# Sixteen quartered pairs of w_up in a row, on sums of its quarters that transfers build in DRAM

## The chip, the cores and the metric

The kernel runs on one core of a Trainium2 chip. The metric is the device time of one execution in microseconds (us). TensorE is PE below, VectorE DVE, ScalarE ACT, GpSimd POOL; SP issues most transfers, and a DMA issued by an engine stands in that engine's order of instructions.

## The reference

One trunk layer of a decoder: x is 512 tokens by 1024 columns, all float32. First attention (a sparse mixer and an RWKV mixer on one combined projection, gated together, an output projection, a residual add), then the channel sub-layer, in which the change lies:

```python
def conv_ffn(h, w_up, conv_w, conv_b, w_down):   # h: 512 x 1024, w_up: 1024 x 5632
    u = h @ w_up
    up = jnp.pad(u, ((0, 0), (CONV_WIDTH - 1, 0), (0, 0)))
    c = conv_b + conv_w[0] * up[:, 0:s]
    for j in range(1, CONV_WIDTH):
        c = c + conv_w[j] * up[:, j:j + s]
    val, gate = jnp.split(c, 2, axis=-1)
    return (jax.nn.silu(gate) * val) @ w_down
```

## The kernel before

Float32 products are made of two parts: a value is split into a rounded high part (an ACT copy) and a low part (value minus high part, a subtraction on DVE or POOL), and a product is three: high by high, high weight by low operand, low weight by high operand.

**The up projection** works on 22 pairs, n = 0 to 21. Pair n has one index f and takes a gate tile and a value tile of 128 columns of w_up (columns 2816 + 128 f and 128 f). A **dense pair** is two `dense_fm` calls of 24 matmuls, each 512 tokens wide. A **quartered pair** (`quartered`) sees the two tiles as a 2 by 2 matrix of quarters: B11 and B12 are the upper 512 rows of w_up for gate and value, B21 and B22 the lower 512. With sums of quarters on both sides seven products do the work of eight; each product is 12 matmuls of 256 tokens. The sums of the tokens' side are made once (`token_sums`, over the first pairs). The weights' side needs T1 = B11 + B12, T2 = T1 + B22, T2 - B11 (which is B12 + B22), and T2 + B21. Before, `wload` loads the upper quarters into two columns of the tile `right` (or a `raw` buffer) and the lower into a `raw` buffer; an adding transfer of POOL (L289) makes T1, and three DVE additions (in `first_quarters` and `quartered`) make the rest. Which pairs are quartered stands in the table `QUARTERED`: n = 5, 6, 8, 9, 11, 12, 14, 15, 17, 18 and 20, two quartered and one dense in turn. After each pair come a causal convolution over tokens (`conv`: one ACT and two DVE instructions for each tile), silu, a product into a column of `right`, and every second pair `sums` for the down projection.

**Buffers.** `right` has 11 columns; columns that hold finished values are copied to DRAM (`kept`, POOL, L1752), lent to the loads, and read back at the end. There are three `raw` buffers, taken in turn, for every weight of the kernel. SP's order of loads is fixed, and a load waits until its buffer is free; a load that waits holds up those behind it.

**Attention** comes first and takes its weights by the same `wload` and `raw` buffers. POOL has work of its own there: low parts of some weight tiles (`wlo<-raw,whi`), some fills (`inv`, whose second half Tn starts a triangular inverse that DVE then runs as a chain), small transfers between partitions (`KH`, `KL`, `Vr`, `sq`). Except in stretches written out by hand, a scheduler fixes each engine's order when the kernel is built.

Of the kernel before, what the change touches and what calls it, by code (L numbers as in the profile page):

```python
# [24 lines left out]
KT = D // 128  # L25
# [58 lines left out]
def hybrid_block(ctx: ExitStack, tc: tile.TileContext, A: dict, out: bass.AP):  # L84
# [133 lines left out]
    hl = hp.tile([128, KT, S], F32R, name="hl", tag="hl")  # L218

    order = [f for i in range(NFH) for f in (i, NFH + i)]  # L220
    QUARTERED = {5: None, 6: 6, 8: 0, 9: 6, 11: 0, 12: 2, 14: 0, 15: 2, 17: 0, 18: 2, 20: 0}

    def weight_tiles():
        def cols(w, o, kt=KT, eng=v):
            return w[:, o:o + 128], kt, 128, eng

        def rows(w, o, n, kt=KT, eng=v):
            step = 1024 // n
            for i, k0 in enumerate(range(0, kt, step)):
                kn = min(step, kt - k0)  # L230
                yield w[128 * k0:128 * (k0 + kn), o:o + n], kn, n, eng[i] if type(eng) is list else eng

        pool_ = nc.gpsimd
        yield cols(w_in, O_RWKV + 1536, eng=pool_)
        yield cols(w_in, O_RWKV + 1664, eng=pool_)
        for p in range(NH2):
            for o in (512, 0, 1024):
                yield cols(w_in, O_RWKV + o + 128 * p)
        yield cols(w_in, O_KC)
        yield from rows(w_in, O_Q, 512, eng=[v, pool_, ("spare", pool_), v])  # L240
        yield cols(w_in, O_VC)
        yield from rows(w_in, O_KS, 256, eng=[v, ("spare", v)])
        for m in range(NGA):
            yield cols(w_in, O_GA + 128 * m)
        yield from rows(w_in, O_KW, 280, eng=pool_)
        for m in range(NGA, KT):
            if m < 4:
                for s4 in range(m if m > NGA else 0, m + 1):
                    for s_ in "kv":
                        yield A["cmp_w1_" + s_][0][512 * s4:512 * s4 + 512], 4, 256, "ab" if (s4, s_) == (3, "k") else None  # L250
            yield cols(w_in, O_GA + 128 * m)
        for m in range(NGB):
            yield cols(w_in, O_GB + 128 * m)
        for m in range(KT):
            if m + NGB < KT:
                yield cols(w_in, O_GB + 128 * (m + NGB), eng=pool_ if m else v)
            yield cols(A["w_proj_b"][0], 128 * m, NH2, eng=pool_)
        for m in range(KT):
            yield cols(A["w_proj_a"][0], 128 * m, NH2)
        yield from rows(A["w_out"][0], 0, 512)  # L260
        yield from rows(A["w_out"][0], 512, 512, eng=())
        for n_, f in enumerate(order):
            if n_ in QUARTERED:
                for kh in range(2):
                    yield A["w_up"][0][512 * kh:512 * kh + 512], KT, 128, ("quarters", f, kh, QUARTERED[n_])
            else:
                yield cols(A["w_up"][0], DFF + 128 * f)
                yield cols(A["w_up"][0], 128 * f)

    wtiles = weight_tiles()  # L270
    loads, ahead, late, behind, spent, slots = [], [], [], [], [], itertools.count()
    def wload():
        nxt = next(wtiles, None)
        if nxt is None:
            if spent:
                spent[0]()
        else:
            src, kt, n, eng = nxt
            if eng == "ab":
                raw, eng = AB[:, 0].rearrange("p a r t -> p (a r t)").rearrange("p (k n) -> p k n", n=n), None  # L280
            elif type(eng) is tuple and eng[:1] == ("quarters",) and not eng[2] and eng[3] is not None:
                raw = right[:, eng[3]:eng[3] + 2].rearrange("p a (k n) -> p (a k) n", n=n)
            else:
                raw = wp.tile([128, kt, n], F32, name="raw", tag=f"raw{next(slots) % 3}", bufs=1)
            if type(eng) is tuple and eng[:1] == ("quarters",):
                for i, c0 in enumerate((DFF + 128 * eng[1], 128 * eng[1])):
                    nc.sync.dma_start(raw[:, 4 * i:4 * i + 4], src[:, c0:c0 + 128].rearrange("(k p) n -> p k n", p=128))
                if not eng[2]:
                    nc.gpsimd.dma_start(raw[:, 4:8], raw[:, 0:4], accum_op=ALU.add)  # L289
                eng = "quarters"  # L290
            else:
                nc.sync.dma_start(raw, src.rearrange("(k p) n -> p k n", p=128))
            loads.append((raw, kt, n, eng))

    def wsplit():
# [8 lines left out]
    def wsplit_():  # L304
        if loads:
# [2 lines left out]
                ahead.append(raw)  # L308
                return
            if eng == "quarters":  # L310
                wload()
                ahead.append(first_quarters(raw, loads.pop(0)[0]))
                return
            if type(eng) is tuple:
                eng = eng[1]
# [1177 lines left out]
    def token_sums():  # L1493
        for kh in range(2):
            def total(o, K, i):
                ks, ns = slice(4 * K + 2 * kh, 4 * K + 2 * kh + 2), slice(256 * i, 256 * i + 256)
                tt(o, hh[:, ks, ns].bitcast(F32), hl[:, ks, ns].bitcast(F32), ALU.add)

            x, y, z, w = [right[:, i].rearrange("p (k n) -> p k n", k=2) for i in range(3, 7)]
            total(x, 0, 1)  # L1500
            total(y, 1, 1)
            tt(y, y, x, ALU.subtract)
            yield
            total(z, 0, 0)
            tt(x, z, x, ALU.subtract)
            stt(z, y, -1.0, z, ALU.mult, ALU.subtract)
            yield
            total(w, 1, 0)
            stt(w, w, -1.0, z, ALU.mult, ALU.subtract)
            for j, o in enumerate((y, z, x, w)):  # L1510
                hi, lo = sum_parts(j, kh)
                act(hi, o)
                tt(lo, o, hi.bitcast(F32), ALU.subtract)
                if j % 2:
                    yield
# [18 lines left out]
    def by_quarter(w):  # L1534
        return w.rearrange("p (q k) n -> p q k n", q=2)

    def first_quarters(top, low):
        b11, t1, b22 = top[:, 0:4], top[:, 4:8], low[:, 4:8]
        hi, lo = two_quarters()
        halves(hi, lo, by_quarter(top))  # L1540
        t2 = pb().rearrange("p (k n) -> p k n", k=4)
        tt(t2, b22, t1, ALU.add)
        tt(b11, t2, b11, ALU.subtract)
        y = 2 * (next(turnsq) % 2)
        t3 = [split[y + j][:, :, NFH - 3].rearrange("p q (k n) -> p q k n", k=2) for j in range(2)]
        halves(*t3, by_quarter(b11))
        return t2, low, (hi, lo), t3

    def quartered():
        t2, low, (h0, l0), (h3, l3) = ahead.pop(0)  # L1550
        b21 = low[:, 0:4]
        G, V, W = mmb(), mmb(), pa()[:, 0:256]
        act(V[:, 0:256], kc[:, 0:256], AF.Copy, scale=0.0)
        U = hB[:, 256 * (NFH + 3):256 * (NFH + 5)]
# [10 lines left out]
            for k in range(4):  # L1565
                mm_on(o, los[k], moving(j, k)[0], False)

        wload()
        h1, l1 = two_quarters()
        with tc.high_priority():  # L1570
            halves(h1[:, 0], l1[:, 0], t2)
            halves(h1[:, 1], l1[:, 1], b21)
        product(W, h0[:, 0], l0[:, 0], -1, True)
        act(G[:, 0:256], W)
        product(V[:, 0:256], h0[:, 1], l0[:, 1], 0)
        act(V[:, 256:512], V[:, 0:256])
        h2, l2 = two_quarters()
        tt(b21, t2, b21, ALU.add)
        halves(h2, l2, by_quarter(low))
        product(W, h1[:, 0], l1[:, 0], 1)  # L1580
        act(U[:, 0:256], W)
# [286 lines left out]
```

## Time and profile before

| | us |
|---|---|
| three runs | 803.55, 803.65, 804.17 |
| median | 803.65 |
| the profiled execution's own time | 803.25 |
| its span, first to last instruction | 801.5 |
| PE busy in it | 794.1 (99%) |
| DVE busy | 641.5 (80%) |
| ACT busy | 468.3 (58%) |
| POOL busy | 79.3 (10%) |

The up projection's quartered stretch lies between 515 and 692 us of the span. Busy time is the time in which an engine had an instruction running; consecutive instructions overlap a little, so what one instruction costs its engine is read from the distance of two starts.

### The profile page before, as it was taken

To read this page: it belongs to the slowest core of one execution; us is meant where nothing else is said; L and a number is where in the kernel's file an instruction comes from. 1 tells how busy PE (TensorE), PEld (TensorE's weight loads), DVE (VectorE), ACT (ScalarE), POOL (GpSimd) and SP (SyncE) were. 2 spreads that over 40 slices of the span, in tenths; PEclk is the share of its full clock that TensorE was granted. 3 is DMA by queue.
4 is the path that set the end of the run, shared out by engine and by line. 5 is a ranking of instruction groups with operands and counts; after the bars stand their busy time and mean duration, and the time that the engine had idled before them with its cause. 6 is when DMAs were issued, how large, how long until landed. Compare 5 with 4: busy or idle time off the path is not lost.

```text
span 801.5 us, 14688 instructions
## 1 busy us (share of the span) xinstructions
PE 794.1 (99%) x5649; PEld 667.3 (83%) x5649; DVE 641.5 (80%) x1240; ACT 468.3 (58%) x958; POOL 79.3 (10%) x115
## 2 busy tenths in 40 slices
PE   8999999999999999999999999999999999999998
PEld 7777788987777887787788898899999999788886
DVE  6477869993665578889685489999999989998895
ACT  6766654563444567778344365576676666546452
POOL 6200011032000044011000000101010000000010
PEclk9999999999999999999999999999999999999999
DMA  8433313237562241000158323574354434676821
GB/s 241 115 79 79 79 53 105 72 81 199 152 108 78 58 91 54 15 27 27 55 181 292 102 69 106 147 194 116 111 153 127 128 82 144 200 245 211 285 96 53
DMA packets 117123, 96.42 MB, mean 120 GB/s; under 512 B 5317, under 2 KB 99452, under 8 KB 116540
## 3 DMA queue, kind: packets, MB, share of 16 engines
q1 hardware_dynamic: 111344, 84.93, 36.7%
q0 software_dynamic: 4656, 8.07, 4.4%
q10 hardware_dynamic: 1052, 2.48, 1.0%
q8 instruction: 44, 0.72, 0.4%
q14 instruction: 27, 0.22, 0.1%
HBM read 84.45 MB, written 6.49 MB: 113 GB/s over the span
## 4 chain that ended last, share of the span: by engine, by line
PE 93%; DVE 3%; ACT 1%; DMA 1%; issue 1%; POOL 0%; DVEq 0%; POOLq 0%; ACTq 0%
PE ps_mm L123 58%; PE ps_mm L126 11%; PE ps_a L126 8%; PE ps_a L123 7%; PE ps_b L123 4%; PE ps_b L126 2%; PE ps_b L1306 1%; DMA pra<-in_rwkv_ln_b_dram 1%; PE ps_mm L1306 1%; DVE P L1232 0%; POOL pra L170 0%; DVE P L136 0%; DVE wlo L132 0%; ACT P L129 0%; ACT whi L129 0%
## 5 line engine op out<-in xcount | busy, mean ns | idle before, releaser
L123 PE MATMUL ps_mm<-hh,whi 128*128 128x512 f32 (+1 forms) x448 | 174.1, 391 | 0.5 <-DVE hl L141 0.5
L129 ACT ACTIVATE whi<-raw 128x1024 fp32r<-128x1024 f32 (+3 forms) x119 | 112.3, 948 | 102.2 <-PE ps_mm L123 66.4
L123 PE MATMUL ps_mm<-hl,whi 128*128 128x512 f32 (+1 forms) x448 | 171.9, 386 | 0.0
L325 DVE TENSOR_TENSOR wlo<-raw,whi 128x1024 fp32r<-128x1024 f32 (+1 forms) x67 | 77.5, 1159 | 40.5 <-ACT whi L129 20.8
L123 PE MATMUL ps_mm<-hh,wlo 128*128 128x512 f32 (+1 forms) x448 | 108.6, 382 | 0.0
L123 PEld LDWEIGHTS ps_mm<-hh,whi 128*128 128x128 f32 x448 | 84.2, 188 | 20.1 <-issue 1.3
L123 PEld LDWEIGHTS ps_mm<-hl,whi 128*128 128x128 f32 x448 | 84.3, 188 | 16.0 <-issue 1.0
L123 PEld LDWEIGHTS ps_mm<-hh,wlo 128*128 128x128 f32 x448 | 82.1, 188 | 16.6
L141 DVE SCALAR_TENSOR_TENSOR right<-ps_mm,cw,right 128x511 f32<-128x511 f32 (+1 forms) x64 | 45.9, 744 | 0.1
L132 DVE TENSOR_TENSOR wlo<-raw,whi 128x1024 fp32r<-128x1024 f32 (+1 forms) x39 | 40.7, 1043 | 5.1 <-ACT whi L129 4.8
L129 ACT ACTIVATE P<-P,nm 128x512 f32<-128x512 f32 (+3 forms) x64 | 35.5, 556 | 11.3 <-DVE nm L1232 10.9
L325 POOL TENSOR_TENSOR wlo<-raw,whi 128x512 fp32r<-128x512 f32 (+3 forms) x13 | 20.9, 1607 | 176.7 <-PE ps_mm L123 142.5
L1232 DVE CUSTOM_DVE_ANT_0 P<-ps_a,AB 128x512 f32<-128x512 f32 (+3 forms) x64 | 29.4, 486 | 1.8 <-PE ps_a L123 1.5
L129 ACT ACTIVATE right<-ps_mm,cw 128x512 f32<-128x512 f32 x32 | 24.0, 770 | 2.5 <-PE ps_mm L123 2.3
L129 ACT ACTIVATE QK<-ps_mm 128x64 f32<-128x64 f32 (+5 forms) x56 | 14.9, 310 | 17.8 <-PE ps_mm L123 17.7
L129 ACT ACTIVATE s<-right 128x512 fp32r<-128x512 f32 (+1 forms) x31 | 16.6, 542 | 12.3 <-DVE right L132 11.6
L123 PE MATMUL ps_mm<-whi,hh 128*128 128x280 f32 (+2 forms) x72 | 22.4, 331 | 0.0
L126 PE MATMUL ps_mm<-hh,whi 128*128 128x256 f32 x88 | 22.1, 283 | 0.0
L126 PE MATMUL ps_mm<-hl,whi 128*128 128x256 f32 x88 | 22.1, 283 | 0.0
L123 PE MATMUL ps_mm<-whi,hl 128*128 128x280 f32 (+2 forms) x72 | 21.8, 323 | 0.0
L129 ACT ACTIVATE whi<-T 128x1024 fp32r<-128x1024 f32 (+1 forms) x12 | 11.9, 993 | 16.6 <-DVE T L132 7.4
L129 ACT ACTIVATE whi<-hA 128x1024 fp32r<-128x1024 f32 (+1 forms) x14 | 13.5, 971 | 13.0 <-PE ps_mm L126 3.7
(497 smaller groups left out, 1980.0 us busy)
## 6 DMA issues: line engine op xcount, KB each, us to landing
raw<-in_w_in_dram SPq DMA_DIRECT2D x38, 512.0 KB, 3.9
raw<-in_w_up_dram SPq DMA_DIRECT2D x22, 512.0 KB, 4.4
raw<-in_w_down_dram SPq DMA_DIRECT2D x18, 512.0 KB, 4.0
raw<-in_w_up_dram SPq DMA_DIRECT2D x24, 256.0 KB, 3.6
hA<-in_w_down_dram SPq DMA_DIRECT2D x12, 512.0 KB, 4.5
right<-in_w_up_dram SPq DMA_DIRECT2D x20, 256.0 KB, 3.0
raw<-in_w_out_dram SPq DMA_DIRECT2D x8, 512.0 KB, 4.4
right<-right POOLq DMA_DIRECT2D x10, 256.0 KB, 4.0
```

Source lines behind the costliest of these rows:

```text
L123: te.matmul(o, lhsT=l, rhs=r, start=start, stop=stop)
L126: te.matmul(o, lhsT=l, rhs=r, start=False, stop=stop, skip_group_check=True)
L129: sc.activation(o, i, f, **kw)
L132: v.tensor_tensor(o, a, b, op=op)
L141: v.scalar_tensor_tensor(o, a, s, b, op0=op0, op1=op1)
L325: low = eng.tensor_tensor(lo, raw, hi.bitcast(F32), op=ALU.subtract)
L1232: maxima.append(v.tensor_tensor_reduce(out=P[:, i], in0=o, in1=BT[:, h, 384 - 128 * qt:512], scale=-1.0, scalar=-NEG, op0=ALU.add, op1=ALU ...
L1306: te.transpose(pt[:, 128 * i:128 * i + 128], P[:, 4 * x + i, 128 * k:128 * k + 128], ident)
```

## The change

- **Quartered pairs.** `QUARTERED` now holds n = 5 to 20, sixteen in a row, with the columns of `right` lent to each.
- **Sums in DRAM.** The sums B12 + B22 (called 3), 3 + B11 (2) and 2 + B21 (4) of the 16 pairs' columns stand in six DRAM tiles of 512 x 1024 (`WSUM`). They are made in 48 pieces of 64 x 1024 (256 KB): a copy from DRAM to DRAM issued by SP right behind a weight load, and at the next load an adding transfer by POOL. `PACE` sets the loads behind which they stand: one piece behind each of loads 8 to 25 and 43 to 48 (counted from 0), two behind each of loads 49 to 60, which are the eight of w_proj_b and the first four of w_proj_a.
- **Loads of a quartered pair.** Seven transfers of 256 KB, not four: B11 and B12 (`top`; POOL still adds T1 there), sum 3 (`third`), sum 2 and B21 (`mid`), sum 4 and B22 (`low`). `mid` and `low` take a `raw` buffer each, `third` one column of `right`.
- **DVE.** The three additions of each quartered pair are gone.
- `token_sums` uses columns 2 to 5 of `right`, not 3 to 6.

```diff
@@ -218,7 +218,9 @@
     hl = hp.tile([128, KT, S], F32R, name="hl", tag="hl")
 
     order = [f for i in range(NFH) for f in (i, NFH + i)]
-    QUARTERED = {5: None, 6: 6, 8: 0, 9: 6, 11: 0, 12: 2, 14: 0, 15: 2, 17: 0, 18: 2, 20: 0}
+
+    QUARTERED = {n: ((0 if n % 2 == 0 else 6 if n < 11 else 2), (4 if n < 9 or 11 < n < 18 else 5 if n < 12 else 7))
+                 for n in range(5, 21)}
 
     def weight_tiles():
         def cols(w, o, kt=KT, eng=v):
@@ -261,11 +263,47 @@
         yield from rows(A["w_out"][0], 512, 512, eng=())
         for n_, f in enumerate(order):
             if n_ in QUARTERED:
-                for kh in range(2):
-                    yield A["w_up"][0][512 * kh:512 * kh + 512], KT, 128, ("quarters", f, kh, QUARTERED[n_])
+                for kind in QUARTER_TILES:
+                    yield f, KT, 128, (kind, n_)
             else:
                 yield cols(A["w_up"][0], DFF + 128 * f)
                 yield cols(A["w_up"][0], 128 * f)
+
+
+    BASE, SPAN = (3, NFH + 2), 1024
+    WSUM = {j: [dp.tile([512, SPAN], F32, name=f"wsum{j}{h}") for h in range(2)] for j in (2, 3, 4)}
+    QUARTER_TILES = {"top": ("B11", "B12"), "third": (3,), "mid": (2, "B21"), "low": (4, "B22")}
+
+    def up_quarter(name, o, n):
+        r, c = 512 * (name[1] == "2"), DFF * (name[2] == "1") + o
+        return A["w_up"][0][r:r + 512, c:c + n]
+
+    def quarter(name, f):
+        if type(name) is str:
+            return up_quarter(name, 128 * f, 128)
+        h = f >= NFH
+        return WSUM[name][h][:, 128 * (f - BASE[h]):128 * (f - BASE[h]) + 128]
+
+    def sum_pieces():
+        for j, x, y in ((3, "B12", "B22"), (2, 3, "B11"), (4, 2, "B21")):
+            for h in range(2):
+                for r in range(0, 512, 64):
+                    a, b = (WSUM[q][h] if type(q) is int else up_quarter(q, 128 * BASE[h], SPAN) for q in (x, y))
+                    yield WSUM[j][h][r:r + 64], a[r:r + 64], b[r:r + 64]
+
+    pieces, adding, event = sum_pieces(), [], itertools.count()
+    PACE = {**{i: 1 for i in (*range(8, 26), *range(43, 49))}, **{i: 2 for i in range(49, 61)}}
+
+    def pace(load):
+        while adding:
+            o, x = adding.pop(0)
+            nc.gpsimd.dma_start(o, x, accum_op=ALU.add)
+        for _ in range(PACE.get(next(event), 0)):
+            o, x, y = next(pieces)
+            copy = nc.sync.dma_start(o, x)
+            tc.add_manual_dep(copy.ins, load.ins.name, mybir.DependencyInfo(
+                mybir.DependencyClass.NoSync, mybir.DependencyReason.DATA), reason="order on one engine")
+            adding.append((o, y))
 
     wtiles = weight_tiles()
     loads, ahead, late, behind, spent, slots = [], [], [], [], [], itertools.count()
@@ -278,18 +316,21 @@
             src, kt, n, eng = nxt
             if eng == "ab":
                 raw, eng = AB[:, 0].rearrange("p a r t -> p (a r t)").rearrange("p (k n) -> p k n", n=n), None
-            elif type(eng) is tuple and eng[:1] == ("quarters",) and not eng[2] and eng[3] is not None:
-                raw = right[:, eng[3]:eng[3] + 2].rearrange("p a (k n) -> p (a k) n", n=n)
+            elif type(eng) is tuple and eng[:1] in (("top",), ("third",)):
+                lent = QUARTERED[eng[1]]
+                raw = (right[:, lent[0]:lent[0] + 2].rearrange("p a (k n) -> p (a k) n", n=n) if eng[0] == "top" else
+                       right[:, lent[1]].rearrange("p (k n) -> p k n", n=n))
             else:
                 raw = wp.tile([128, kt, n], F32, name="raw", tag=f"raw{next(slots) % 3}", bufs=1)
-            if type(eng) is tuple and eng[:1] == ("quarters",):
-                for i, c0 in enumerate((DFF + 128 * eng[1], 128 * eng[1])):
-                    nc.sync.dma_start(raw[:, 4 * i:4 * i + 4], src[:, c0:c0 + 128].rearrange("(k p) n -> p k n", p=128))
-                if not eng[2]:
+            if type(eng) is tuple and eng[:1] and eng[0] in QUARTER_TILES:
+                for i, q in enumerate(QUARTER_TILES[eng[0]]):
+                    nc.sync.dma_start(raw[:, 4 * i:4 * i + 4], quarter(q, src).rearrange("(k p) n -> p k n", p=128))
+                if eng[0] == "top":
                     nc.gpsimd.dma_start(raw[:, 4:8], raw[:, 0:4], accum_op=ALU.add)
-                eng = "quarters"
+                    eng = "quarters"
             else:
-                nc.sync.dma_start(raw, src.rearrange("(k p) n -> p k n", p=128))
+                load = nc.sync.dma_start(raw, src.rearrange("(k p) n -> p k n", p=128))
+                pace(load)
             loads.append((raw, kt, n, eng))
 
     def wsplit():
@@ -308,8 +349,9 @@
                 ahead.append(raw)
                 return
             if eng == "quarters":
-                wload()
-                ahead.append(first_quarters(raw, loads.pop(0)[0]))
+                while len(loads) < len(QUARTER_TILES):
+                    wload()
+                ahead.append(first_quarters(raw, *(loads.pop(0)[0] for _ in range(len(QUARTER_TILES) - 1))))
                 return
             if type(eng) is tuple:
                 eng = eng[1]
@@ -1496,7 +1538,7 @@
                 ks, ns = slice(4 * K + 2 * kh, 4 * K + 2 * kh + 2), slice(256 * i, 256 * i + 256)
                 tt(o, hh[:, ks, ns].bitcast(F32), hl[:, ks, ns].bitcast(F32), ALU.add)
 
-            x, y, z, w = [right[:, i].rearrange("p (k n) -> p k n", k=2) for i in range(3, 7)]
+            x, y, z, w = [right[:, i].rearrange("p (k n) -> p k n", k=2) for i in range(2, 6)]
             total(x, 0, 1)
             total(y, 1, 1)
             tt(y, y, x, ALU.subtract)
@@ -1534,21 +1576,16 @@
     def by_quarter(w):
         return w.rearrange("p (q k) n -> p q k n", q=2)
 
-    def first_quarters(top, low):
-        b11, t1, b22 = top[:, 0:4], top[:, 4:8], low[:, 4:8]
+    def first_quarters(top, third, mid, low):
         hi, lo = two_quarters()
         halves(hi, lo, by_quarter(top))
-        t2 = pb().rearrange("p (k n) -> p k n", k=4)
-        tt(t2, b22, t1, ALU.add)
-        tt(b11, t2, b11, ALU.subtract)
         y = 2 * (next(turnsq) % 2)
         t3 = [split[y + j][:, :, NFH - 3].rearrange("p q (k n) -> p q k n", k=2) for j in range(2)]
-        halves(*t3, by_quarter(b11))
-        return t2, low, (hi, lo), t3
+        halves(*t3, by_quarter(third))
+        return mid, low, (hi, lo), t3
 
     def quartered():
-        t2, low, (h0, l0), (h3, l3) = ahead.pop(0)
-        b21 = low[:, 0:4]
+        mid, low, (h0, l0), (h3, l3) = ahead.pop(0)
         G, V, W = mmb(), mmb(), pa()[:, 0:256]
         act(V[:, 0:256], kc[:, 0:256], AF.Copy, scale=0.0)
         U = hB[:, 256 * (NFH + 3):256 * (NFH + 5)]
@@ -1565,17 +1602,17 @@
             for k in range(4):
                 mm_on(o, los[k], moving(j, k)[0], False)
 
-        wload()
+        for _ in range(len(QUARTER_TILES) - 1 if loads[0][3] == "quarters" else 1):
+            wload()
         h1, l1 = two_quarters()
         with tc.high_priority():
-            halves(h1[:, 0], l1[:, 0], t2)
-            halves(h1[:, 1], l1[:, 1], b21)
+            halves(h1[:, 0], l1[:, 0], mid[:, 0:4])
+            halves(h1[:, 1], l1[:, 1], mid[:, 4:8])
         product(W, h0[:, 0], l0[:, 0], -1, True)
         act(G[:, 0:256], W)
         product(V[:, 0:256], h0[:, 1], l0[:, 1], 0)
         act(V[:, 256:512], V[:, 0:256])
         h2, l2 = two_quarters()
-        tt(b21, t2, b21, ALU.add)
         halves(h2, l2, by_quarter(low))
         product(W, h1[:, 0], l1[:, 0], 1)
         act(U[:, 0:256], W)
```

Three places show how instructions moved.

**POOL, in attention, at the projection of q** (`wlo` and `spare` are low parts of weight tiles, `inv` holds Tn, `wsum` are the DRAM sums). Before:

```order
L325 TENSOR_TENSOR wlo<-raw,whi 128x1024
L640 MEMSET inv 128x1024
L641 MEMSET inv 128x32
L325 TENSOR_TENSOR spare<-raw,spare 128x1024
L880 MEMSET kc 128x256
L736 MEMSET QK 1x8
```

With the change:

```order
L367 TENSOR_TENSOR wlo<-raw,whi 128x1024
L300 DMA wsum_105<-in_w_up_dram 64x1024 x2
L367 TENSOR_TENSOR spare<-raw,spare 128x1024
L682 MEMSET inv 128x1024
L922 MEMSET kc 128x256
L683 MEMSET inv 128x32
L300 DMA wsum_105<-in_w_up_dram 64x1024 x3
L778 MEMSET QK 1x8
```

Two adding transfers, each of which waits for its copy, now stand ahead of `spare`, and the fills of `inv` behind it.

**DVE, one quartered pair in the middle of the stretch.** Before:

```order
L132 TENSOR_TENSOR wlo<-ps_b,whi 128x512
L132 TENSOR_TENSOR wlo<-raw,whi 128x512
L141 SCALAR_TENSOR_TENSOR right<-ps_mm,cw,right 128x511 x2
L141 SCALAR_TENSOR_TENSOR right<-ps_mm,cw,right 128x510 x2
L132 TENSOR_TENSOR raw<-ps_b,raw 128x512
L132 TENSOR_TENSOR right<-right 128x512
L132 TENSOR_TENSOR hB<-right 128x256
L132 TENSOR_TENSOR wlo<-raw,whi 128x1024
```

With the change:

```order
L132 TENSOR_TENSOR wlo<-raw,whi 128x512 x2
L141 SCALAR_TENSOR_TENSOR right<-ps_mm,cw,right 128x511 x2
L141 SCALAR_TENSOR_TENSOR right<-ps_mm,cw,right 128x510 x2
L132 TENSOR_TENSOR wlo<-raw,whi 128x1024
L132 TENSOR_TENSOR right<-right 128x512
L132 TENSOR_TENSOR hB<-right 128x256
L132 TENSOR_TENSOR wlo<-right,whi 128x1024
```

The addition `raw<-ps_b,raw` is gone, and no low part is taken from the PSUM tile `ps_b` that held T2.

**SP, late in the stretch.** Before, a quartered pair and the dense one after it:

```order
L287 DMA right<-in_w_up_dram 128x4x128 x2
L287 DMA raw<-in_w_up_dram 128x4x128 x4
L292 DMA raw<-in_w_up_dram 128x8x128
```

With the change, two quartered pairs:

```order
L327 DMA right<-wsum_105 128x4x128
L327 DMA raw<-wsum_106 128x4x128
L327 DMA raw<-in_w_up_dram 128x4x128
L327 DMA raw<-wsum_103 128x4x128
L327 DMA raw<-in_w_up_dram 128x4x128
L327 DMA right<-in_w_up_dram 128x4x128 x2
L327 DMA right<-wsum_104 128x4x128
L327 DMA raw<-wsum_107 128x4x128
L327 DMA raw<-in_w_up_dram 128x4x128
```

The order of PE's instructions in attention is the same in both kernels.

## Rows read from the trace of the kernel before

**Rows 1.** The page: PE's busy time; the chain's shares by engine.

```profile
PE 794.1 (99%) x5649; PEld 667.3 (83%) x5649; DVE 641.5 (80%) x1240; ACT 468.3 (58%) x958; POOL 79.3 (10%) x115
...
PE 93%; DVE 3%; ACT 1%; DMA 1%; issue 1%; POOL 0%; DVEq 0%; POOLq 0%; ACTq 0%
```

**Rows 2.** The chain in order of time: start us, length us, what.

```profile
547.04 1.32 PE ps_a L126 x11
548.36 1.44 PE ps_mm L126 x12
...
557.12 1.32 PE ps_a L126 x11
...
567.08 10.91 PE ps_mm L123 x48
```

**Rows 3.** Windows: length; PE, PEld, DVE, ACT, POOL busy; PEclk; DMA share; GB/s.

```profile
547.04:671.28 124.24, 124.24 (x866) 116.66 (x866) 117.15 (x184) 83.46 (x154) 8.93 (x12) 1.00 0.44 119
502.00:505.00 3.00, 3.00 (x15) 2.49 (x14) 3.00 (x6) 1.97 (x3) 0.00 (x0) 1.00 0.92 262
180.00:200.00 20.00, 20.00 (x240) 15.49 (x241) 6.12 (x18) 6.08 (x21) 6.31 (x11) 1.00 0.73 193
```

**Rows 4.** Timeline of DVE: start us, length us, instruction.

```profile
131.31 0.21 DVE L141 SCALAR_TENSOR_TENSOR Tm<-inv 128x31 f32<-128x31 f32 x1
...
549.89 0.68 DVE L132 TENSOR_TENSOR raw<-ps_b,raw 128x512 f32<-128x512 f32 x1
550.49 0.69 DVE L132 TENSOR_TENSOR right<-hB,right 128x512 f32<-128x512 f32 x1
...
552.01 1.22 DVE L132 TENSOR_TENSOR wlo<-raw,whi 128x1024 fp32r<-128x1024 f32 x1
553.14 0.42 DVE L132 TENSOR_TENSOR hB<-right,hB 128x256 f32<-128x256 f32 x1
...
558.60 2.72 DVE L141 SCALAR_TENSOR_TENSOR right<-ps_mm,cw,right 128x511 f32<-128x511 f32 x4
561.23 0.69 DVE L132 TENSOR_TENSOR raw<-ps_b,raw 128x512 f32<-128x512 f32 x1
```

**Rows 5.** DMA issues: count, KB each, median us from issue to landing.

```profile
right<-right POOLq DMA_DIRECT2D x10, 256.0 KB, 4.0
...
raw<-in_w_proj_b_dram SPq DMA_DIRECT2D x8, 256.0 KB, 2.8
...
kept<-right POOLq DMA_DIRECT2D x8, 256.0 KB, 2.9
...
AB<-vd SPq DMA_DIRECT2D x8, 128.0 KB, 9.1
```

**Rows 6.** Timeline of POOL.

```profile
120.55 0.95 POOL L640 MEMSET inv<- 128x1024 f32 x1 [1.39 <-PE ps_a L123]
121.56 0.16 POOL L641 MEMSET inv<- 128x32 f32 x1
121.71 2.42 POOL L325 TENSOR_TENSOR spare<-raw,spare 128x1024 fp32r<-128x1024 f32 x1
124.08 0.30 POOL L880 MEMSET kc<- 128x256 f32 x1
...
287.43 0.51 POOL L1076 DMA_DIRECT2D KL<-KL  x1 [1.42 <-DVE rs_y L141]
...
378.75 1.29 POOL L325 TENSOR_TENSOR wlo<-raw,whi 128x512 fp32r<-128x512 f32 x1 [7.12 <-ACT P L129]
...
549.55 0.86 POOL L289 DMA_DIRECT2D right<-right  x1 [16.98 <-DVE s L132]
```

**Rows 7.** Timeline of SP: load 19 (w_in, counted from 0).

```profile
119.18 0.37 SPq L292 DMA_DIRECT2D raw<-in_w_in_dram  x1
```

**Rows 8.** Timeline of PE: first use of KH; low part of the last w_proj_b tile.

```profile
298.52 0.48 PE L123 MATMUL ps_a<-KH,qst 128*128 128x512 f32 x1
...
390.42 0.86 PE L123 MATMUL ps_mm<-obT,wlo 128*128 128x512 f32 x3
```

## The prediction

> **What bounds the kernel now.** I read the page first. PE is busy for 794.1 of 801.5 us, and 93% of the chain that ended last is PE work [rows 1]; DVE has 80%, POOL 10%. So time can only leave where PE gets less work, and can only come where PE is made to wait. The reader should see that no gain on DVE or POOL counts by itself here.
>
> Next the chain in order of time, inside the up projection, gives the price of a pair. A quartered pair begins with a group of 11 matmuls on `ps_a`. One begins at 547.04 and the next at 557.12 [rows 2]: one quartered pair is 10.08 us. The row behind the first shows a full product, 12 matmuls in 1.44, and seven of them are 10.08 as well, so nothing is lost between products. The dense pair is one row of 48 matmuls of 10.91 us [rows 2].
>
> Then the windows, for what else is near its limit. Over the 12 pairs from 547.04 to 671.28 (8 quartered, 4 dense) PE is busy for all of 124.24 us, DVE for 117.15, and the DMA engines have a share of 0.44 at 119 GB/s [rows 3]. The reader should see that DVE stands 6% behind PE, so the stretch has two bounds close together, and that the transfers have room.
>
> **The sum, part by part.** *PE.* Five pairs (n = 7, 10, 13, 16, 19) change from dense to quartered, at 10.91 - 10.08 = 0.83 us each: **-4.15 us**. PE's order in attention does not change, so nothing else moves there unless something is late.
>
> *DVE in the stretch.* Each old quartered pair loses three additions of 128x512. Such an operation runs 0.60 us from start to start (549.89 to 550.49) [rows 4], so 8 x 3 x 0.60 = 14.4 us go, and 117.15 becomes 102.75. A dense pair that turns quartered gains the three 128x512 combinations of products (3 x 0.60, as `right<-hB,right` shows) and 0.61 us of smaller pieces (the `hB<-right,hB` kind, and low parts cut in halves). Estimate 2.4 us for each of four, together 9.6. That is 112.35 us in 12 pairs, **9.36 us per pair** against PE's 10.08. The old idle time, 124.24 - 117.15 = 7.09 over 12 pairs, is 0.59 each; with it DVE would need 9.95, which still fits. I take no cost. What covers DVE is PE's own length, with 0.13 us to spare beyond the old idle time; without that cover each missing tenth costs 1.6 us over 16 pairs. The four convolution instructions, 2.72 us together, and the low parts of 128x1024, 1.13 each [rows 4], are the same in both.
>
> *Transfers in the stretch.* A quartered pair now issues seven loads of 256 KB (1.835 MB), its adding transfer (0.262) and, in pairs whose finished column is stored, a copy of 0.131 on average: 2.23 MB in 10.08 us, 221 GB/s. The stretch had 119 GB/s at a share of 0.44, so about 270 at a full share, and 221 would be a share near 0.82. The trace reaches 262 GB/s at 0.92 between 502 and 505 us, but only 193 at 0.73 between 180 and 200 us [rows 3]; those are the two ends. A load of such rows lands 2.8 us after its issue and the adding transfer 4.0 [rows 5], and the buffers are taken about a pair ahead for `mid`, `low` and `top`, and about 8 us ahead for `third`. So I take no cost, and keep the end at 193 GB/s as a rival. SP issues three more transfers in such a pair than before, at about 0.37 each [rows 7]: 2.6 us of 10.08 in all, alone on its engine. The adding transfer keeps its 0.86 us on POOL [rows 6], which has 8.93 us of work in 124.24 there [rows 3].
>
> *Attention.* It gains 48 copies and 48 adding transfers, 2 x 48 x 0.262 = 25 MB. On SP that is 48 x 0.37 = 18 us, on POOL 48 x 0.86 = 41 us, next to 79.3 us busy. Neither engine bounds anything as a whole. But POOL's adding transfer waits for its copy, and what stands behind it on POOL waits too. The trace of before shows no copy from DRAM to DRAM; its landing is bounded by `kept<-right`, 2.9 us, as the same size to DRAM, and by `AB<-vd`, 9.1 us, the slowest read from DRAM [rows 5]. I take 2.9, the nearer in size and rows. Three places matter:
>
> 1. Load 19 is issued at 119.18 for 0.37 [rows 7], so its copy goes at 119.55 and lands at 119.92 + 2.9 = 122.8. Behind it on POOL stand an add (0.86), `spare` (2.42) and the fills (0.95, 0.30, 0.16) [rows 6]: done at 127.5. DVE's chain takes Tn (`Tm<-inv`) at 131.31 [rows 4]. Slack 3.8 us; with a landing of 9.1 the chain would be 2.4 us late.
> 2. `KH` and `KL` are issued until 287.43 [rows 6]; PE first takes KH at 298.52 [rows 8], more than 10 us later.
> 3. The low part of a w_proj_b tile, the last at 378.75 to 380.04 [rows 6], now has two adds ahead; PE takes it at 390.42 [rows 8]. Two copies and two adds (2.9 + 2 x 0.86, and 9.1 + 1.7 at worst) fit into 10 us or nearly.
>
> Two further 256 KB transfers between successive weight loads take 1.0 to 1.4 us each of all DMA engines (262 and 193 GB/s); loads run ahead of their use, so again I take 0. The price of attention is thus 0, and its range 0 to +2.4, the worst of these three places.
>
> A rule of the Trainium skill speaks against the adds (the page "SBUF — State Buffer", the section "Who interferes with whom"): VectorE's two-port operations lock GpSimd out, so its descriptors, and with them its DMAs, start late, about 620 ns becoming about 3100 ns. The rows: in a stretch where DVE is busy 94% of the time [rows 3], an adding transfer's issue took 0.86 us on POOL [rows 6]. By that rule the five adds around `inv` would take 3.1 each; the one ahead of the fills then puts them at about 129.7, an estimate, still ahead of 131.31. Hence its chance stays within the second case below.
>
> *Sum.* The profiled execution took 803.25 (span 801.5 and 1.75 around it): 803.25 - 4.15 = 799.10. The median of the three runs lies 0.40 above that execution, so **799.5 us**. Reading starts to 0.1 us over five pairs gives 0.5, the spread of runs (803.55 to 804.17) 0.6, and a small first wait of the new order may add as much: 798.2 to 800.8 for this case alone. A difference under 0.2%, 1.6 us (802.0 to 805.3), can't be told from none.
>
> **The rivals.**
>
> *As forecast, or a little better* (0.65): DVE 9.4, DMA share near 0.8, no wait on POOL. 799.5.
>
> *POOL is late in attention* (0.11): a copy lands in 9 us, so Tn, or a `wlo` in the third place, holds PE. For it: POOL takes instructions in order and the adds wait at the head. Against: the slack of 3.8 and 10 us. 799.5 + 2.4 = 801.9.
>
> *DVE becomes the bound* (0.14): its work per pair fits with 0.72 us idle, and decides beyond that. For it: if the whole old idle time of 7.09 us stood in the eight quartered pairs it is 0.89 each, and 9.36 + 0.89 = 10.25; every second pair also carries `sums`. Then 16 x 0.17 = 2.7, and 799.5 + 2.7 = 802.2. Against: for 3 us after 502 DVE was busy in all of them while PE was too [rows 3], so idle time is not needed.
>
> *The transfers don't keep up* (0.10), the other side: 16 pairs in a row have no dense one in which the queue recovers, and a load that waits for a buffer holds up those behind it. It decides where 2.23 MB takes as long as makes the gain vanish, 10.34 us per pair (10.08 + 4.15/16), 216 GB/s sustained. At the 193 GB/s of 180 to 200 us a pair takes 11.55, 1.47 longer: 16 x 1.47 = +23.5, thus 803.65 + 23.5 - 4.15 = 823.0. For it: small blocks of 128 columns, and 221 GB/s that has to hold for 160 us where the trace shows 262 for 3. Against: 193 came at a share of 0.73, so was not the limit.
>
> That the sums aren't ready, so that the change doesn't do what it says, would show as a wait of `third` at n = 5; the last pieces go with the first tiles of w_proj_a, soon after the last low part of w_proj_b at 378.75 [rows 6], and the stretch begins at 515, so I give it nothing apart.
>
> **How the numbers follow.** The likeliest case gives 799.5. The range from 798.2 to 802.9 holds the first three cases with the last one's spread of 0.7 above 802.2; outside stay the transfers' 0.10 and the remainder of the others, some 0.1. Faster by over 0.2%: 0.65 + 0.11 = 0.76; within: 0.14; slower: 0.10.
>
> **What would show it.** In the profile after: quartered pairs starting 10.08 us apart, sixteen in a row, PE without gaps; DVE busy near 93% of the stretch, a DMA share near 0.8 at about 220 GB/s, each load landing 3 to 5 us after its issue; `Tm<-inv` still at 131.3; PE's order reaching 515 us as before. Gaps before the products on `third` or `low`, with SP's queue as what ended them, would make the transfers right; gaps with DVE busy throughout, DVE; a shift already before 400 us, POOL.

## The result and the profile after

The changed kernel took a median of **807.96 us** over 15 runs, the kernel before 803.67 over its own 15: slower by 0.54% (95% interval 0.44% to 0.64%). The forecast was 799.5, between 798.2 and 802.9. The runs also spread as those of before don't: 803.95 to 811.91, against 803.38 to 804.20. Two of its executions were profiled: one of 805.67 us, whose rows are shown here, and one of 804.86 (e1_repeat below, where eight executions of the same kernel had a median of 805.80).

The page of the profile after has these lines for [rows 1]:

```profile
PE 790.4 (98%) x5829; PEld 672.5 (84%) x5829; DVE 635.9 (79%) x1227; ACT 485.2 (60%) x1003; POOL 122.0 (15%) x168
...
PE 86%; DVE 6%; DMA 3%; ACT 3%; issue 1%; POOL 0%; DVEq 0%; ACTq 0%; POOLq 0%; SPq 0%
```

PE works 3.7 us less than before, near the first term of the forecast (-4.15; e8 below measures it). But the chain now runs over DVE, DMA and ACT for longer: PE waits. The list of what PE waited for begins with three rows that the kernel before doesn't have (us in total, times, longest):

```profile
PE ps_a L123 <- DVE nm L1274: 2.3, 1, 2.3
PE ps_a L126 <- ACT hB L129: 1.8, 2, 1.3
PE ps_a L126 <- ACT ps_mm L129: 1.3, 1, 1.3
```

Where they lie is read from the starts of the quartered pairs (the first matmul of each pair, from the timeline of PE). Pair 5 starts at 517.77, and at 515.48 before: **+2.29 us of attention**. From there to the start of pair 20 there are 15 pairs; at 10.08 each they would take 151.20, and they take 155.47. The distances are 10.08 to 0.01 but for four: 10.44 (pair 5), 11.64 and 11.69 (pairs 11 and 12) and 10.82 (pair 17): **+4.27 us in the stretch**. From there to the end it is 130.4 us, against 130.5 before. So 803.25 + 2.29 - 4.15 + 4.27 = 805.66, and the execution took 805.67.

The window over these 15 pairs answers to [rows 3] (length; PE, PEld, DVE, ACT, POOL busy; PEclk; DMA share; GB/s):

```profile
517.77:673.24 155.47, 152.21 (x1262) 151.39 (x1260) 139.01 (x216) 119.73 (x233) 16.48 (x21) 1.00 0.80 210
```

DVE needs 139.01 / 15 = 9.27 us per pair, and the transfers have a share of 0.80: both as forecast, and neither the bound.

**The wait in pair 11**, from the chain in order of time:

```profile
574.03 0.65 DVE right L132
574.68 0.29 issue
574.97 3.74 DMA kept<-right
578.72 0.02 SPq L327
578.74 0.03 issue
578.77 4.32 DMA right<-wsum
...
583.65 1.04 ACT whi L129
584.69 0.52 ACT right L129
585.21 0.27 ACT ps_mm L129
585.48 0.31 ACT hB L129
585.79 0.04 issue
585.84 1.70 PE ps_a L126 x12
```

DVE finishes a column of pair 9 (column 4). POOL stores it (`kept`), which takes 3.74 us to land, and only then may SP load `third` of pair 12 into it, because `QUARTERED` lends pair 12 the column 4; another 4.32 us. ACT's order is fixed. The high part of that `third` stands there ahead of the copy of pair 11's product out of PSUM (`hB`), so a load for the next pair holds up this one. Pair 17 has the same chain (`third` of pair 18 in column 7, finished by pair 15):

```profile
638.63 4.05 DMA kept<-right
...
642.73 3.18 DMA right<-wsum
```

In pairs 5 and 12 no copy is involved: there consecutive pairs are lent the same column (4), and each `third` is issued only when the low part of the one before it has been taken (behind the low parts of pairs 6, 7 and 8 the next loads go at 517.02, 521.73 and 527.19), so a late one makes the next one late as well. ACT's row for it in pair 12 (in brackets the idle time before it, and what ended it):

```profile
591.30 0.63 ACT L129 ACTIVATE s<-right 128x512 fp32r<-128x512 f32 x1 [2.22 <-DMA right<-wsum]
```

**The wait in attention**, on POOL and on DVE, near 311 us:

```profile
309.95 1.68 POOL L300 DMA_DIRECT2D wsum<-in_w_up_dram  x2
311.03 1.13 POOL L1163 DMA_DIRECT2D Vr<-vt  x1
311.58 1.88 POOL L367 TENSOR_TENSOR wlo<-raw,whi 128x512 fp32r<-128x512 f32 x1
...
310.89 0.17 DVE L132 TENSOR_TENSOR sm<-sm,gts 128x4 f32<-128x4 f32 x1
311.09 2.67 DVE L136 TENSOR_SCALAR P<-P,sm 128x512 f32<-128x512 f32 x1
...
314.41 0.50 PE L123 MATMUL ps_a<-KH,qst 128*128 128x512 f32 x1 [2.31 <-DVE nm L1274]
```

The same place in the kernel before:

```profile
308.75 1.30 POOL L325 TENSOR_TENSOR wlo<-raw,whi 128x512 fp32r<-128x512 f32 x1
...
310.70 0.16 DVE L132 TENSOR_TENSOR sm<-sm,gts 128x4 f32<-128x4 f32 x1
310.89 0.49 DVE L136 TENSOR_SCALAR P<-P,sm 128x512 f32<-128x512 f32 x1
```

Before, POOL's low part ended at 310.05, 0.65 us ahead of DVE's `sm`. With adds among POOL's small transfers it comes 2.8 us later and runs beside DVE. A DVE instruction of 0.49 us takes 2.67 and ends at 313.76, 0.30 us behind POOL's low part. Its row begins 0.49 us ahead of that low part but 0.06 behind POOL's issue of `Vr`, so POOL's issues are part of what it runs beside.

The Trainium skill has this direction too (the page "SBUF — State Buffer", the section "Who interferes with whom"): a VectorE instruction with two SBUF inputs and a GpSimd instruction that reads SBUF exclude each other, one in a two-port mode and GpSimd do so as well, and the order of issue decides who waits. The rows of e2 and e7 below agree on the order; that a shared port is the reason is the page's, and no run here shows it by itself.

### The profile page after: what moved, and what is told of

Read it like the earlier page. It is cut to its first block, busy times and chain, and to the rows that moved or that the text cites. A ratio compares the mean times of both kernels' runs of the same rounds, so it can differ in the third digit from the quotient of the medians.

```text
span 803.6 us, 15422 instructions
## 1 busy us (share of the span) xinstructions
PE 790.4 (98%) x5829; PEld 672.5 (84%) x5829; DVE 635.9 (79%) x1227; ACT 485.2 (60%) x1003; POOL 122.0 (15%) x168
## 4 chain that ended last, share of the span: by engine, by line
PE 86%; DVE 6%; DMA 3%; ACT 3%; issue 1%; POOL 0%; DVEq 0%; ACTq 0%; POOLq 0%; SPq 0%
PE ps_mm L123 51%; PE ps_mm L126 11%; PE ps_a L126 8%; PE ps_a L123 7%; PE ps_b L123 4%; PE ps_b L126 2%; DMA right<-wsum 2%; DVE wlo L132 1%; DMA kept<-right 1%; PE ps_b L1348 1%; ACT whi L129 1%; DVE P L136 1%; DMA pra<-in_rwkv_ln_b_dram 1%; PE ps_mm L1348 1%; DVE s L132 0%
## 5 line engine op out<-in xcount | busy, mean ns | idle before, releaser
L129 ACT ACTIVATE whi<-raw 128x512 fp32r<-128x512 f32 (+2 forms) x134 | 117.7, 891 | 101.0 <-PE ps_mm L123 57.9
L123 PE MATMUL ps_mm<-hh,whi 128*128 128x512 f32 (+1 forms) x368 | 142.9, 392 | 0.3 <-DVE hl L141 0.3
L123 PE MATMUL ps_mm<-hl,whi 128*128 128x512 f32 (+1 forms) x368 | 140.7, 386 | 0.0
L367 DVE TENSOR_TENSOR wlo<-raw,whi 128x1024 fp32r<-128x1024 f32 (+1 forms) x57 | 65.3, 1147 | 38.8 <-PE ps_mm L123 21.4
L123 PE MATMUL ps_mm<-hh,wlo 128*128 128x512 f32 (+1 forms) x368 | 88.8, 380 | 0.0
L123 PEld LDWEIGHTS ps_mm<-hh,wlo 128*128 128x128 f32 x368 | 67.1, 188 | 13.5
L300 POOL DMA_DIRECT2D wsum<-in_w_up_dram x48 | 39.2, 859 | 230.7 <-DMA wsum<-wsum 116.6
L132 DVE TENSOR_TENSOR wlo<-raw,whi 128x512 fp32r<-128x512 f32 (+1 forms) x64 | 58.5, 935 | 11.0 <-ACT whi L129 11.0
L329 POOL DMA_DIRECT2D right<-right x16 | 13.9, 870 | 188.7 <-DVE right L132 76.4
L126 PE MATMUL ps_mm<-hh,whi 128*128 128x256 f32 x128 | 32.2, 284 | 0.1
```

The costliest lines, as they stand in the source:

```text
L123: te.matmul(o, lhsT=l, rhs=r, start=start, stop=stop)
L126: te.matmul(o, lhsT=l, rhs=r, start=False, stop=stop, skip_group_check=True)
L129: sc.activation(o, i, f, **kw)
L132: v.tensor_tensor(o, a, b, op=op)
L300: nc.gpsimd.dma_start(o, x, accum_op=ALU.add)
L367: low = eng.tensor_tensor(lo, raw, hi.bitcast(F32), op=ALU.subtract)
```

## The experiments

Theories: **C**, columns that come free too late; **P**, POOL's work holding up DVE in attention; **T** (the rival of the forecast), DMA engines that don't keep up in the stretch; **K**, a clock that falls behind a wait; **D**, the pieces' bytes delaying POOL's small transfers; **F**, instructions that reach PE late while the DMA engines are full. Each run is compared with the kernel before, run beside it on the same chip (803.56 us for e1 to e4, 803.21 for e5, e6, e7 and e8, 803.73 for e9). In e4, e7 and e8 sums or parts of them are left out, so those runs serve for their times alone.

| run | columns | building | median us | against before, 95% |
|---|---|---|---|---|
| e1_repeat | as changed | as changed | 805.80 | 1.0038 (1.0022 to 1.0054) |
| e2_thirds | new | as changed | 801.60 | 0.9983 (0.9972 to 0.9993) |
| e3_build_only | kernel before | as changed | 807.11 | 1.0041 (1.0029 to 1.0054) |
| e4_no_build | as changed | none | 804.54 | 1.0016 (1.0006 to 1.0026) |
| e5_later | new | loads 53 to 64 | 807.62 | 1.0051 (1.0039 to 1.0063) |
| e6_pace | new | none at 49-52, 59-62 | 802.87 | 0.9997 (0.9985 to 1.0009) |
| e7_sp_traffic | new | adds at 49-52 as SP copies | 801.37 | 0.9976 (0.9968 to 0.9985) |
| e8_thirds_no_build | new | none | 799.05 | 0.9946 (0.9934 to 0.9959) |
| e9_pace2 | new | none at 49-52, 59-64 | 799.37 | 0.9954 (0.9939 to 0.9969) |

**e1_repeat**: the changed kernel, no edit.

> The changed kernel as it is, for a second profile. The first profile (805.67 us, granted clock 1.000) lost 2.31 us to one wait near 314 us and 4.27 us in the quartered stretch at three places (pairs 5, 11 and 12, 17); 15 runs had a median of 807.96. Theory C (columns: `third` is lent a column that comes free too late): the same three places in the stretch, 3.5 to 5 us in all, whatever the time of the run. Theory K (clock): where the time is nearer 808, the granted clock is under 1.000 in some stretch behind a wait, and the rest of the time is lost there, 2 us or more. Rival T (the transfers don't keep up at 221 GB/s): waits at other places of the stretch than these three, and a mean pair over 10.4 us.

The profiled execution took 804.86. The same four pairs are long (10.65, 10.57, 11.99 and 10.68: +3.57), and pair 5 starts 2.16 us late: 803.25 + 2.16 - 4.15 + 3.57 = 804.83. The places are C's, not T's. This execution was one of the shorter of its eight (804.35 to 809.86), so K stays untested here. In attention PE waits at the same place, 1.42 us, behind another DVE instruction (`sm<-sm,gts`, 1.41 us where it takes 0.16 before).

**e2_thirds**: other columns for `third`, nothing else.

```diff
+    THIRD = {5: 4, 6: 5, 7: 4, 8: 5, 9: 4, 10: 5, 11: 6, 12: 7, 13: 6, 14: 7, 15: 4, 16: 5, 17: 4, 18: 5, 19: 6, 20: 7}
-    QUARTERED = {n: (..., (4 if n < 9 or 11 < n < 18 else 5 if n < 12 else 7)) for n in range(5, 21)}
+    QUARTERED = {n: (..., THIRD[n]) for n in range(5, 21)}
```

> Only the columns lent to `third` change: 4, 5, 4, 5, 4, 5, 6, 7, 6, 7, 4, 5, 4, 5, 6, 7 for pairs 5 to 20, so that none is lent the column of the pair before it or one that was finished two or three pairs earlier. Theory C: the 4.27 us in the stretch go, every pair starts 10.1 us after the last, and the median falls from about 808 to 803.7, or to 801.5 if what the other runs lose beyond the profiled one hangs on the stretch too. Rival T: `third` waits less and other loads of the pair wait instead, pairs of 10.3 us or more, 806 to 808.

Its window over the same 15 pairs:

```profile
517.89:669.08 151.19, 151.19 (x1262) 151.19 (x1260) 138.94 (x215) 119.03 (x232) 16.48 (x21) 1.00 0.81 216
```

PE is without a gap, every distance is 10.07 or 10.08, and all 4.27 us are back; by medians it is 4.20 (805.80 in e1, 801.60 here). C is shown and T is out: the DMA engines carry 216 GB/s for 150 us and PE never waits. The profiled execution took 801.52, and 803.25 + 2.41 (pair 5 late) - 4.15 = 801.51: what is left is attention alone. There PE waits 0.96 us at the old place:

```profile
310.30 1.68 POOL L300 DMA_DIRECT2D wsum<-in_w_up_dram  x2
...
311.93 1.90 POOL L367 TENSOR_TENSOR wlo<-raw,whi 128x512 fp32r<-128x512 f32 x1
...
310.81 0.99 DVE L132 TENSOR_TENSOR sm<-sm,gts 128x4 f32<-128x4 f32 x1
311.83 0.49 DVE L136 TENSOR_SCALAR P<-P,sm 128x512 f32<-128x512 f32 x1
```

Here `sm` (0.16 us before) takes 0.99 and ends 0.13 us before the low part begins: what it ran beside were POOL's issues of transfers alone. `P` began 0.10 us ahead of the low part and kept its 0.49, and the low part took 1.90, not 1.30. So the collision is not with the low part only. And PE waits at a new place:

```profile
391.34 0.27 PE L123 MATMUL ps_b<-PTs,Vr 32*64 32x64 f32 x2 [1.39 <-issue]
...
390.00:392.00 2.00, 0.66 (x63) 0.66 (x67) 0.00 (x0) 0.00 (x0) 0.00 (x0) 1.00 1.10 382
```

"issue" is time in which PE waited for nothing that the profile shows. It stands in a dense run of small matmuls, and (second row, a window) while the DMA engines are full with two pieces. Theory F is that the instructions themselves came late; what the traces have on that stands below, under what stays open.

**e3_build_only**: the kernel before with the building alone (`WSUM`, `sum_pieces`, `PACE` and `pace` as in the change); nothing reads the sums.

```diff
-                nc.sync.dma_start(raw, src.rearrange("(k p) n -> p k n", p=128))
+                load = nc.sync.dma_start(raw, src.rearrange("(k p) n -> p k n", p=128))
+                pace(load)
```

> The kernel before, with the 48 copies and 48 adding transfers in their places during attention, and nothing that reads the sums. Theory P (POOL's adding transfers and low parts hold up a DVE instruction at 311 us): 2.3 us slower than before, 806, with one wait of PE near 312 to 315 us on `nm`; 808 if the part that the profile of the change does not show (2.3 us of the median) is lost in attention too. If attention costs nothing, as I had forecast: 803.7, and the 2.3 us were a chance of the one profile.

3.55 us slower than before: building costs this much by itself, where I had forecast 0. PE waits 2.25 us on `nm` at 314.37. And behind that wait the granted clock falls (windows; the column ahead of the DMA share):

```profile
300.00:312.00 12.00, 11.91 (x60) 9.52 (x59) 10.67 (x34) 9.58 (x24) 10.17 (x18) 1.00 0.55 131
312.00:316.00 4.00, 1.75 (x6) 1.31 (x5) 3.47 (x6) 2.38 (x7) 4.00 (x9) 0.82 1.04 249
316.00:320.00 4.00, 4.00 (x28) 2.33 (x26) 3.05 (x11) 2.48 (x6) 3.16 (x4) 0.75 0.82 174
320.00:324.00 4.00, 4.00 (x27) 3.24 (x26) 2.72 (x7) 1.83 (x4) 0.00 (x0) 1.00 0.95 178
```

0.18 x 4 + 0.25 x 4 = 1.7 us of full clock are missing. Pair 5 starts at 519.75, 4.27 us late, in the main 2.25 of wait, 1.7 of clock and 0.36 of a wait on "issue" at 393. This is K: nearly the same wait cost 2.3 us in the first profile and 4 here. It is one part of the spread of the runs, not all of it (see what stays open).

**e4_no_build**: `PACE` is empty, and a sum's load reads a quarter of w_up.

```diff
-    PACE = {**{i: 1 for i in (*range(8, 26), *range(43, 49))}, **{i: 2 for i in range(49, 61)}}
+    PACE = {}
-        h = f >= NFH
-        return WSUM[name][h][:, 128 * (f - BASE[h]):128 * (f - BASE[h]) + 128]
+        return up_quarter({3: "B22", 2: "B12", 4: "B21"}[name], 128 * f, 128)
```

> The change without the copies and the adding transfers of attention; the seven loads of a quartered pair stay, but those of the sums read quarters of w_up, so the sums are left out of the product. Theory C: -4.15 for the five pairs and +4.27 for the three places, 803.8, with the same three places in the profile. If the 2.3 us that the median has beyond the profile belong to the stretch: 806. Theory P alone (the stretch would be well without the building): 799.5.

804.54: without any building the stretch alone takes back all the gain, and 0.98 more. The profiled execution, 802.50, was the shortest of the eleven, which reach 808.01. In it pair 5 starts at 515.32, as before, and the distances have the same four long ones (10.43, 10.81, 12.00, 10.84: +3.76). The two us between that profile and the median have no profile.

**e8_thirds_no_build**: the edits of e2 and e4 together.

```diff
+    QUARTERED = {n: (..., THIRD[n]) for n in range(5, 21)}
+    PACE = {}
```

> The columns of e2_thirds without any building in attention; loads of sums read quarters of w_up instead, so the sums are left out of the product. Theory C, and the first term of the forecast: exactly -4.15, pairs of 10.08 and no wait that the kernel before does not have, 799.4 (799.0 to 799.9), as steady as the kernel before. Rival T: still some tenths lost in the stretch, 800.5 or more.

799.05, from 798.85 to 799.22 over 5 runs: 4.16 us under before, the forecast's term of -4.15, and steady. So the term was right, and the stretch can hold it. The wide spread is gone with both causes; either alone brings it (e4, without building, 802.50 to 808.01; e2, with good columns, 800.73 to 804.74).

**e5_later**: on e2, the pieces of loads 49 to 52 behind 61 to 64.

```diff
-    PACE = {..., **{i: 2 for i in range(49, 61)}}
+    PACE = {..., **{i: 2 for i in range(53, 65)}}
```

> As e2_thirds (801.6), with two pieces behind each of loads 53 to 64 and none behind 49 to 52, so that POOL issues no adding transfer between its small transfers (`Vr`, `sq`) near 300 to 320 us. Theory P (POOL busy without a break holds up DVE): no DVE instruction of 0.2 to 0.5 us takes over 1 us near 311, PE's wait of 0.96 to 2.31 us on `nm` near 314 goes, and the median falls by 1 to 2.5, to 799.5 to 800.5. Rival D (the copies' load on the DMA engines delays the small transfers, not POOL): they are gone from there too, so the same. Theory F (PE waited 1.39 us near 391 for its instructions while the DMA engines were full): that wait stays in some runs, since pieces still stand there.

The wait on `nm` is gone, and DVE's instructions near 311 have their old lengths; P and D both say so. "issue" is there (1.20 us at 390). But the median is 6 us higher, which no theory expected. From the chain:

```profile
403.78 11.29 DMA raw<-in_w_proj_a_dram
...
415.86 9.16 PE ps_mm L123 x32
...
410.00:415.00 5.00, 2.06 (x10) 1.36 (x8) 0.54 (x1) 0.00 (x0) 0.00 (x0) 1.00 1.07 277
415.00:420.00 5.00, 4.14 (x12) 3.33 (x13) 4.06 (x6) 3.16 (x5) 1.59 (x2) 0.71 0.96 305
```

The last tile of w_proj_a lands 11.29 us after its issue, with pieces ahead of and beside it. PE waits 3.80 us, and the clock is 0.71 behind it. There the weights were needed soon after their load, and there the DMA engines are full (1.07).

**e6_pace**: the same pieces partly behind the early loads.

```diff
+    PACE = {**{i: 1 for i in (*range(16, 26), *range(43, 49))}, **{i: 2 for i in (*range(8, 16), *range(53, 59), 63, 64)}}
```

> As e2_thirds, with two pieces behind each of loads 8 to 15, one behind 16 to 25 and 43 to 48, two behind 53 to 58, 63 and 64; none behind 49 to 52 or 59 to 62. P and F both: neither the wait near 314 nor that near 391; PE reaches the first quartered pair at 515.5 us as in the kernel before, the median is 799.5, and the runs lie within 1 us of each other. If twice the pieces behind loads 8 to 15 hold up loads: a wait of PE between 40 and 120 us, 800.5 or more.

In its profile (800.80, the shortest of its runs) the waits near 314 and 391 are gone, and behind loads 8 to 15, with two pieces each, no new wait stands. One wait of over 0.25 us, 0.82 at 414.31, is left, on a load of w_out behind the pieces of loads 63 and 64. Pair 5 starts at 517.15, not 515.5, and the median of 802.87, up to 806.25, missed the expectation as well.

**e7_sp_traffic**: on e2, the eight adds of loads 49 to 52 as plain copies on SP.

```diff
+            if 49 <= e <= 52:
+                copies.append(nc.sync.dma_start(other[r:r + 64], y))
+            else:
                 adding.append((o, y))
...
```

> As e2_thirds, but behind loads 49 to 52 the eight adding transfers of POOL become plain copies of the same bytes issued by SP into a DRAM tile that nothing reads, so eight pieces of a sum lack their second term. POOL has nothing of the building near 311 us; the DMA engines have the same bytes. Theory P: the wait near 314 goes as in e5_later, and the median is about 800. Rival D: the wait of 1 to 2.3 us near 314 stays, 801.6.

Neither theory alone: the wait stays, 0.81 us (0.96 in e2), though POOL has no add there. Its rows:

```profile
307.30 2.27 POOL L1170 DMA_DIRECT2D Vr<-vt  x4 [0.79 <-DMA Vr<-vt]
...
310.56 1.29 POOL L374 TENSOR_TENSOR wlo<-raw,whi 128x512 fp32r<-128x512 f32 x1
...
311.04 0.84 DVE L132 TENSOR_TENSOR sm<-sm,gts 128x4 f32<-128x4 f32 x1
```

POOL's small transfers wait for each other, and these land later beside the pieces (`Vr` takes a median of 3.8 us to land, 2.2 before); so the low part slips to 310.56 and meets DVE. POOL's low part is first here and keeps its 1.29 us, and `sm`, issued 0.48 later, ends 0.03 behind it. The collision of POOL's work with DVE's is the price, and both the adds and the bytes can push POOL into it. The median is level with e2's (801.37 and 801.60).

**e9_pace2**: e6 with its last four pieces behind loads 20 to 23.

```diff
+    PACE = {**{i: 1 for i in (*range(16, 20), 24, 25, *range(43, 49))}, **{i: 2 for i in (*range(8, 16), *range(20, 24), *range(53, 59))}}
```

> As e6_pace (802.87, whose profile waits 0.82 us near 414 behind a load that shares the DMA engines with the pieces of loads 63 and 64), with those four pieces behind loads 20 to 23 instead; so none behind 49 to 52 or 59 to 64. Theory P with F and D (each wait of attention is a piece in the wrong place): no wait that the kernel before lacks, 799.5, the runs within 1 us of each other like e8_thirds_no_build (799.05). If the building costs something wherever it stands: 801 or more, with waits at new places.

799.37 us, 4.36 under before, with the full computation. The profiled execution took 798.81, pair 5 starts at 515.41, and the window over the pairs has no gap:

```profile
515.41:666.61 151.20, 151.20 (x1262) 151.19 (x1261) 138.99 (x215) 119.12 (x232) 16.48 (x21) 1.00 0.81 216
```

PE has no wait of 0.25 us or more that the kernel before lacks. Of six runs five lie between 798.67 and 800.08; one took 803.05, at a mean clock of 0.998. Against before that is as much as without any building (4.16 in e8), so building costs nothing that shows where it stands well; a rare wait is not ruled out.

## Why the prediction was wrong

- **PE, -4.15**: right. e8 measured -4.16.
- **DVE, 9.36 us per pair**: right; 9.27 measured, and PE has no gap in e2.
- **Transfers, a share near 0.82, 221 GB/s**: right, 0.81 and 216. The rival that ended on the slower side was wrong in its mechanism; the DMA engines kept up.
- **The step that failed first**: "the buffers are taken about a pair ahead for `mid`, `low` and `top`, and about 8 us ahead for `third`. So I take no cost". The 8 us were taken for every pair alike. For pairs 12 and 18 the lent column is one that the pair three ahead of it has just finished, so storing it (3.74 us) and loading (4.32) come first. Pairs 5 to 8 and 12 to 17 share one column in turn, so a late load delays the next; sharing by itself cost nothing where no load was late (pairs 13 to 16 start 10.08 apart). It cost 4.27 us in the profile (e2 gives it back), and took the whole gain.
- **The step that failed second**: "The price of attention is thus 0, and its range 0 to +2.4". It cost 2.29 us in the first profile, and 3.55 as a median (e3). The term for a copy's landing, 2.9 us, was too small as well: copies took 4.3 to 4.8. Even so the three places that I weighed held: the fills ended at 130.1 in the profile after (forecast 127.5) and the chain on Tn began at 131.5, and PE is not late at the other two. I had looked for those who take what POOL makes. The wait came from one who takes nothing of it: DVE, which had run 0.65 us behind a low part of POOL.
- **The rule of the skill** that I weighed is one half of its section: VectorE locking out GpSimd. What held PE up was the other direction, DVE late beside POOL. The figure of 3100 ns is the page's for a whole transfer (its section "A bandwidth-pool intuition that's wrong (but worth ruling out)"), not for an issue; here an adding transfer's issue took 0.78 us on POOL, its median in the profile after.
- **What stays open**: the median of the changed kernel lies 2.3 us over its first profile, and none of its longer executions was profiled. The clock is part of that: of the 15 executions the four at a mean granted clock of 1.000 took 803.95 to 807.89 us, the other eleven, at 0.995 to 0.998, 806.60 to 811.91. Waits of other lengths would account for the rest. So the sizes are less sure than the places: by medians the columns cost 4.20 (e1 less e2) to 5.14 (e4 less e8, each against its kernel before), the building 1.26 (e1 less e4) to 3.55 (e3). Why the clock fell behind some waits and not behind others stays open too.
- **The wait on "issue" near 390** (e2, e3, e5 and e7, not in e6 and e9, which have no pieces there). The transfers of the queue called `instruction` in the DMA view speak for F. In the kernel before one of 16 KB starts at 386.57, and PE takes the instruction that waits in e2 at 388.93, 1.25 us behind that transfer's end. Measured by PE's own progress the same transfer starts 1.45 us late in e2, 0.54 in e3, 1.36 in e5 and 1.55 in e7, and the waits are 1.39, 0.36, 1.20 and 1.48; in the other profiles it is within 0.2 us of its place, and no such wait is over 0.2. In all of them PE goes on 1.25 to 1.46 us behind its end. That the pieces make it late is argued: no run moved it alone. The changed kernel and e1 have pieces there as well and no such wait; in them it started at 388.96 and 388.80, when the DMA share (388 to 390) was still 0.54 and 0.57, against 1.02 in e2.

## What to carry to other kernels

When a buffer is lent from a pool, its slack is that of the tightest user, not of the usual one: list for each use who frees the buffer and when, and count a store to DRAM and a load from it in full. Work on an idle engine is free only where its neighbours' order keeps; look also at which other engine slows down beside it, above all where the two ran a fraction of a microsecond apart before. And background transfers belong where no load is needed soon after its issue.

## What was not expected of the hardware

- A DVE instruction of 0.49 us took 2.67, and one of 0.16 took 0.84 to 1.41, beside POOL's low part; in e2 the second took 0.99 beside POOL's issues of transfers alone.
- Waits of PE of 2.25, 3.80 and 1.48 us (e3, e5, e7) were followed by a granted clock at the lower of its two levels, 1.2 of 2.4 GHz, for a stretch: the mean was 0.79 over 312 to 320 us, 0.83 over 415 to 425 and 0.83 over 392 to 402, 1.7 us of full clock each time. Behind waits of 2.31, 1.42 and 1.39 us (the first profile, e1, e2) it stayed at 1.00. So one wait has two prices.
- A load of 256 KB that lands in 2.8 us in the kernel before (the median of w_proj_b [rows 5]) took 11.29 in e5, with six copies of 256 KB issued from 6 us ahead of it to 2 behind, and six adds beside them.
- Copies from DRAM to DRAM landed in 4.3 to 4.8 us (medians of the profile after), and the adding ones in 4.6, with 0.78 us of issue on POOL.
